# A hybrid attention and HGRN2 layer: weight differences, q and k evictions and output weights put at other places in the engines' order

## The chip, the cores and the metric

The kernel runs on one core of one Trainium2 chip. The time is the device time of one launch in microseconds (us); three runs of the kernel before gave 1321.59, 1317.43 and 1322.69, median 1321.59. The engines are called PE (TensorE, matmuls), PEld (its weight loads), DVE (VectorE), ACT (ScalarE), POOL (GpSimd) and SP (SyncE, which here issues the DMAs).

## The reference

One decoder layer over 1040 tokens (16 meta tokens ahead of 1024), model width 1024, float32:

```python
a = rmsnorm(h, ln_mix_pre[l])
proj = a @ w_in[l]
dq, dk, dv, hq, hf, hi, hg = jnp.split(proj, SPLITS, axis=-1)
y_diff = diff_attention(dq, dk, dv, ...)      # 4 heads: softmax(q0 k0) - lam * softmax(q1 k1), times v, rmsnorm
y_hgrn = hgrn2(hq, hf, hi, hg, ...)           # 4 heads of gated linear recurrence
mix = jnp.concatenate([y_diff, y_hgrn], axis=-1) @ w_out[l]
h = h + rmsnorm(mix, ln_mix_post[l])
a = rmsnorm(h, ln_ffn_pre[l])
y = conv_ffn(a, w_ffn_up[l], ffn_conv_w[l], ffn_conv_b[l], w_ffn_down[l])   # width 2816, causal conv of 3
h = h + rmsnorm(y, ln_ffn_post[l])
```

The output is h without the meta tokens.

## The kernel before

Every float32 operand of a large product is split into a high and a low part in a faster format, and a product is three matmuls (high·high, high·low, low·high). The feed-forward part uses a Strassen-like scheme with fewer products of 512-wide halves; for that it needs differences of pieces of `w_down`, which are made early, beside the projections, and kept in DRAM (`tsc`).

The tokens are nine blocks: one of 16 and eight of 128, in three groups (`GROUPS`, 272, 384 and 384 tokens). The input projection is 28 tiles of 128 columns, each a set of three groups. Tiles named `dq`, `dk`, `dv` feed an attention head, `hq`, `hf`, `hi`, `hg` an HGRN2 head. While the projection of the next head runs, the current head is computed: `interleave` takes steps of the head (a generator that yields a cost) and fills PE between them with projection matmuls. Attention heads 0 to 3 and HGRN2 heads 0 to 3 alternate. After HGRN2 head 3 comes the output projection with `w_out`, in two column halves, the first of them beside HGRN2 head 3 (`out_first`); then the feed-forward part, to the end.

PE executes in the order in which the program is written. The other engines are put in order by a scheduler, which goes by the order of writing as a priority and by when it thinks operands are ready. Two means restrict it: `tc.keep_in_program_order`, which the class `Ordered` applies to DVE's and ACT's instructions while `state["ordered"]` is set, and `with tc.issue_after(ins)`, which puts what stands in the block behind `ins` on its engine. All DVE and ACT instructions go through `Ordered`, so that the profile gives them one line, L54; they are told apart by tile names.

The names that matter here:

- `down_sums` (L195 on) is a generator advanced once for each projection group. For each of 11 rounds it loads four 128x512 pieces of `w_down` (`wd11`, `wd12`, `wd22`, `wd21`, in a pool of five buffers), makes four differences on DVE (`wd3` = 22 − 12, then 12, 22 and 21 in place), and stores each to `tsc` by SP.
- `ev_q` and `ev_k` evict a PSUM bank of the q or k projection (`pi_dq`, `pi_dk`, two banks in turn): ACT writes the scaled or rounded copy, DVE the remainder. For k the remainder goes to a tile `kl`, and ACT writes a second copy into the other half of the partitions.
- `attn` runs, for each block i, the scores (`scores`), the transposes of its softmax weights `pb` into `at` (`values`, matmuls on L693) and their product with v (`apply`, L717).
- In an HGRN2 head, level 1 to 7 of a tree each need `mix` and `kr` scaled by DVE (`mix<-mix,tt`, `kr<-kr,tt`) before their matmuls `pl<-mix,kr` on L459; `a` and `am` receive the masked result.
- `load_wo` loads a 128x512 piece of `w_out` into a buffer `wor` (three in turn) and splits it: a cast on ACT (`wh` or `woh`), the remainder on DVE (`wl` or `wol`). `mm` are the split activations of the output projection, `py` its sums.

Of the kernel before, what the change touches and what calls it, by code (L numbers as in the profile page):

```python
# [13 lines left out]
ALU = mybir.AluOpType  # L14
# [8 lines left out]
KD = D // P  # L23
# [3 lines left out]
NBLK = 9  # L27
# [18 lines left out]
class Ordered:  # L46
# [3 lines left out]
    def __getattr__(self, name):  # L50
        call = getattr(self.engine, name)

        def issue(*args, **kw):
            ins = call(*args, **kw)  # L54
            return self.tc.keep_in_program_order(ins) if self.state["ordered"] else ins

        return issue
# [29 lines left out]
def layer_kernel(ctx: ExitStack, tc: tile.TileContext, x, meta, table, lbl, gpre, gpost, win,  # L87
# [3 lines left out]
    V, A = Ordered(tc, nc.vector, state), Ordered(tc, nc.scalar, state)  # L91
# [56 lines left out]
    def ps_m(name):  # L148
        return pp.tile([P, 512], F32, tag="m", name=name)
# [4 lines left out]
    def split(hi, lo, raw, eng=None):  # L154
        A.copy(hi, raw)
        (eng or G).tensor_tensor(lo, raw, hi.bitcast(F32), op=ALU.subtract)
# [38 lines left out]
    def down_sums():  # L195
        def load(k):
            with tc.issue_after(last_load[-1].ins):
                for nm, kk, half in (("11", k, 0), ("12", k, 1), ("22", k + NF // 2, 1), ("21", k + NF // 2, 0)):
                    b[nm] = wsp.tile([P, 512], F32, tag="wd", name=f"wd{nm}_{k}")
                    SY.dma_start(b[nm], wdown[P * kk: P * (kk + 1), 512 * half: 512 * (half + 1)])  # L200
            b["t3"] = wsp.tile([P, 512], F32, tag="wd", name=f"wd3_{k}")

        b = {}
        load(0)
        yield
        yield
        for k in range(NF // 2):
            for j, d, p_, q_ in ((2, "t3", "22", "12"), (0, "12", "12", "11"), (1, "22", "22", "12"), (3, "21", "21", "22")):
                V.tensor_tensor(b[d], b[p_], b[q_], op=ALU.subtract)
                with tc.issue_after(last_load[-1].ins):  # L210
                    SY.dma_start(tsc[j][P * k: P * (k + 1)], b[d])
                yield
            if k + 1 < NF // 2:
                load(k + 1)
                yield

    def up_raw(ft, nm):
# [374 lines left out]
    def attn_in(h):  # L592
        qs = [ap_.tile([P, L], F32R, tag=f"q{m}", name=f"q{m}_{h}") for m in range(2)]
        ks = [ap_.tile([P, L], F32R, tag=f"k{m}", name=f"k{m}_{h}") for m in range(2)]
        vn = ap_.tile([P, NBLK, P], F32, tag="avn", name=f"avn{h}")
        G.memset(vn[:, 0], 0.0)
        rr = ap_.tile([P, 256], F32, tag="rr", name=f"rr{h}")
        own = [slice(0, 64), slice(64, 128)]
        oth = [slice(64, 128), slice(0, 64)]

        def ev_q(g, b0, b1, t0, t1, pt):
            for m in range(2):
                A.mul(qs[m][own[m], t0:t1], pt[own[m]], 0.125)
                V.scalar_tensor_tensor(qs[m][oth[m], t0:t1], pt[own[m]], 0.125, qs[m][own[m], t0:t1].bitcast(F32), ALU.mult, ALU.subtract)

        def ev_k(g, b0, b1, t0, t1, pt):
            for m in range(2):
                A.copy(ks[m][own[m], t0:t1], pt[own[m]])
                V.tensor_tensor(kl[m][own[m], t0:t1], pt[own[m]], ks[m][own[m], t0:t1].bitcast(F32), op=ALU.subtract)
                A.copy(ks[m][oth[m], t0:t1], pt[own[m]])  # L610

        def ev_v(g, b0, b1, t0, t1, pt):
            vt = ap_.tile([P, 384], F32, tag="vt", name=f"vt{h}_{g}", bufs=1)
            A.copy(vt[:, : t1 - t0], pt)
            late.append((vn, vt, b0, b1, f"va{h}_{g}"))

        return (qs, ks, vn, rr), [(h, f"dq{h}", ev_q), (4 + h, f"dk{h}", ev_k), (8 + h, f"dv{h}", ev_v)]

    def attn(h, tens):
        qs, ks, vn, rr = tens  # L620
# [115 lines left out]
        for i in range(NBLK):  # L736
            if i + 2 < NBLK:
                ahead = scores(i + 2)
                yield next(ahead)
            yield from apply(i)  # L740
            if i + 2 < NBLK:
                yield from ahead
            if i + 2 == NBLK:
                yield 2
            if i + 1 < NBLK:
                yield from values(i + 1)
        carry.append(pend.pop("tail"))
# [42 lines left out]
    pt = ps_m("pg")  # L790
# [80 lines left out]
    for c in range(2):  # L871
        raw = wp.tile([P, 512], F32, tag="wr", name=f"wr3_{c}", bufs=3)
# [61 lines left out]
    FIRST = (2, 3, 4, 5, 6, 7, 8, 1)  # L934
    kept = kpp.tile([P, 2, KD, P], F32R, tag="kept", name="kept")

    def load_wo(n, k):
        raw = wp.tile([P, 512], F32, tag="wr", name=f"wor{n}_{k}", bufs=3)
        last_load.append(SY.dma_start(raw, wout[P * k: P * (k + 1), 512 * n: 512 * (n + 1)]))
        if k < 2:  # L940
            where, tag, bufs = wp, ("wh", "wl"), 4
        elif n == 0 and k < KD - 1:
            where, tag, bufs = w0p, ("woh", "wol"), KD - 3
        else:
            where, tag, bufs = w1p, ("woh", "wol"), KD - 1
        hi, lo = (where.tile([P, 512], F32R, tag=t, name=f"{t}{n}_{k}", bufs=bufs) for t in tag)
        split(hi, lo, raw, V if n or k else G)
        return hi, lo
# [41 lines left out]

    sps = [mix_split(i, 0, 4) for i in FIRST[:2]]
    mix_split(0, 0, 7)
    wo0 = [load_wo(0, k) for k in range(KD)]
    wo = []

    pre_last = {}
# [27 lines left out]
    def out_first():  # L1024
        pys = [ps_s(f"py0_{i}")[:, 0] for i in FIRST[:2]]
        for ks in ((0, 1), (2, 3)):
            for j in range(2):
                yield from out_part(sps[j], pys[j], wo0, ks[0] == 0, False, ks)
        sqs = [mix_split(i, 4, 7) for i in FIRST[:2]]
        for j in range(2):  # L1030
            yield from out_part(sqs[j], pys[j], wo0, False, True)
            if j == 0:
                sp_ = mix_split(FIRST[2], 0, 4)
            A.copy(y0[:, FIRST[j]], pys[j])
        for n, i in enumerate(FIRST[2:]):
            for k in ((0, 1), (2, 3), (4,), (5,), (6,), (7,))[n]:
                wo.append(load_wo(1, k))
            if n == 3:
                ahead.extend(mix_load(2, c) for c in range(4))
            py = ps_in(f"py0_{i}")  # L1040
            sq_ = mix_split(i, 4, 7)
            yield from out_part(sp_, py, wo0, True, False)
            if i != FIRST[-1]:
                sp_ = mix_split(FIRST[n + 3], 0, 4)
            yield from out_part(sq_, py, wo0, False, True)
            A.copy(y0[:, i], py)
        py = ps_in("py0_0")
        yield from out_meta(py, wo0, 0, 7, 6)
        A.copy(y0[:2, 0], py[32:34])
        V.tensor_tensor(y0[:2, 0], y0[:2, 0], py[:2], op=ALU.add)  # L1050
        while 0 not in finished:
            yield None
        for p in range(3):
            pre_last[p] = mix_split(p, 7, 8)
        for p in range(3):
            yield from out_last(p)
# [171 lines left out]
    for n, i in enumerate(order):  # L1228
# [9 lines left out]
        nxt = []  # L1238
# [521 lines left out]
```

## Time and profile before

| | before |
|---|---|
| median of three runs | 1321.59 us |
| the profiled execution: its own time | 1323.17 us |
| its span | 1321.4 us |
| PE busy | 1273.0 us, 96% |
| DVE busy | 920.0 us, 70% |
| ACT busy | 689.2 us, 52% |
| POOL busy | 419.0 us, 32% |

A row of the timeline gives the start in us from the span's start, the length, engine, source line, operation, output tile <- input tiles, shapes, and how many were grouped; in brackets how long the engine stood idle before it and whose result ended that. A row of the waits gives an engine's instruction, what it waited for, the sum in us, how often, and the longest. A row by windows gives the stretch and its length, then for each engine its busy time with the number of instructions.

The projection with heads beside it takes the first 500 us or so; the output projection lies up to about 560 us; the feed-forward part, which the change does not touch, follows.

### The profile page before, as it was taken

How to read it: one execution, taken by the hardware profiler on the slowest of the kernel's cores; microseconds unless marked ns; L12 is line 12 of the kernel's file. 1: busy time of each engine (PE TensorE's matmuls, PEld its weight loads, DVE VectorE, ACT ScalarE, POOL GpSimd, SP SyncE). 2: the span in 40 equal slices, each digit the busy share in tenths (PEclk: the TensorE clock that was granted, in tenths of full speed). 3: DMA queues.
4: the chain of work that ended last, by engine and by line, in shares of the span. 5: the costliest groups of instructions: out<-in, count | busy, mean ns of one | idle time of the engine just before them, and what ended most of it. 6: DMA issues, size and time to landing. Idle time of an engine off the chain costs nothing.

```text
span 1321.4 us, 26287 instructions
## 1 busy us (share of the span) xinstructions
PE 1273.0 (96%) x10212; PEld 1180.3 (89%) x10212; DVE 920.0 (70%) x1591; ACT 689.2 (52%) x1671; POOL 419.0 (32%) x325
## 2 busy tenths in 40 slices
PE   6999999999999999999999989999999999999997
PEld 5898899989999999777899989999999998888886
DVE  7566556564756465746889877877787875697587
ACT  7365346535654565456655444455454453554454
POOL 3211211121202120113156757667666641010021
PEclk9999999999999999999999989999999999999999
DMA  6331323142311111836613222222222325964363
GB/s 218 106 130 61 100 93 129 61 129 80 122 44 35 33 33 49 255 112 206 226 41 113 89 80 88 80 83 79 81 89 80 105 81 163 355 216 155 109 207 120
DMA packets 84371, 153.07 MB, mean 116 GB/s; under 512 B 9571, under 2 KB 19843, under 8 KB 84246
## 3 DMA queue, kind: packets, MB, share of 16 engines
q1 hardware_dynamic: 84246, 151.39, 34.6%
q8 instruction: 80, 1.31, 0.4%
q14 instruction: 45, 0.37, 0.1%
HBM read 112.69 MB, written 38.67 MB: 115 GB/s over the span
## 4 chain that ended last, share of the span: by engine, by line
PE 64%; DVE 7%; issue 2%; ACT 2%; DMA 2%; SPq 0%; POOL 0%; DVEq 0%; ACTq 0%; POOLq 0%
PE pd L1571 5%; PE pd L1572 5%; PE pd L1570 5%; PE pb L1360 4%; PE pb L1361 4%; PE pb L1362 4%; PE pa L1361 2%; PE pa L1360 2%; PE pa L1362 2%; PE pc L1362 2%; PE pc L1360 2%; PE pc L1361 2%; DVE c L54 2%; PE py L978 2%; PE pa L717 2%
## 5 line engine op out<-in xcount | busy, mean ns | idle before, releaser
L1360 PE MATMUL pb<-t,uh 128*128 128x258 f32 (+1 forms) x480 | 135.7, 283 | 10.3 <-DVE u L54 10.3
L1361 PE MATMUL pb<-t,uh 128*128 128x258 f32 (+1 forms) x480 | 135.2, 282 | 0.0
L1362 PE MATMUL pb<-t,ul 128*128 128x258 f32 (+1 forms) x480 | 135.1, 281 | 0.0
L1572 PE MATMUL pd<-wh,gl 128*128 128x512 f32 (+1 forms) x314 | 121.0, 385 | 0.0
L1571 PE MATMUL pd<-wl,gh 128*128 128x512 f32 (+1 forms) x314 | 120.5, 384 | 0.4 <-DVE wl L54 0.3
L1570 PE MATMUL pd<-wh,gh 128*128 128x512 f32 (+1 forms) x314 | 120.8, 385 | 0.0
L54 DVE SCALAR_TENSOR_TENSOR c<-uu,cwt,c 128x512 f32<-128x512 f32 x88 | 96.5, 1097 | 19.8 <-ACT c L54 19.2
L1306 POOL TENSOR_TENSOR c<-c,c 128x512 f32<-128x512 f32 x44 | 67.6, 1536 | 118.4 <-ACT c L54 112.3
L1360 PEld LDWEIGHTS pb<-t,uh 128*128 128x128 f32 x480 | 91.5, 191 | 11.1 <-DVE u L54 11.1
L54 DVE SCALAR_TENSOR_TENSOR c<-ug,cwt,c 128x512 f32<-128x512 f32 x88 | 89.8, 1020 | 2.9 <-ACT c L54 2.3
L1361 PEld LDWEIGHTS pb<-t,uh 128*128 128x128 f32 x480 | 91.6, 191 | 0.0
L1362 PEld LDWEIGHTS pb<-t,ul 128*128 128x128 f32 x480 | 91.5, 191 | 0.0
L1361 PE MATMUL pa<-t,uh 128*128 128x258 f32 (+1 forms) x320 | 89.9, 281 | 0.0
L1360 PE MATMUL pa<-t,uh 128*128 128x258 f32 (+1 forms) x320 | 89.8, 281 | 0.0
L1362 PE MATMUL pa<-t,ul 128*128 128x258 f32 (+1 forms) x320 | 89.8, 280 | 0.0
L1362 PE MATMUL pc<-t,ul 128*128 128x256 f32 x320 | 88.3, 276 | 0.0
L1360 PE MATMUL pc<-t,uh 128*128 128x256 f32 x320 | 88.3, 276 | 0.0
L1361 PE MATMUL pc<-t,uh 128*128 128x256 f32 x320 | 88.3, 276 | 0.0
L1571 PEld LDWEIGHTS pd<-wl,gh 128*128 128x128 f32 x314 | 58.9, 188 | 14.1 <-DVE wl L54 1.6
L1572 PEld LDWEIGHTS pd<-wh,gl 128*128 128x128 f32 x314 | 59.0, 188 | 12.1
L1570 PEld LDWEIGHTS pd<-wh,gh 128*128 128x128 f32 x314 | 59.0, 188 | 11.5
L54 ACT ACTIVATE pb<-S,ast 128x528 f32<-128x528 f32 (+7 forms) x72 | 46.6, 648 | 39.2 <-DVE ast L54 39.1
(411 smaller groups left out, 4210.8 us busy)
## 6 DMA issues: line engine op xcount, KB each, us to landing
ra<-in_wup_dram SPq DMA_DIRECT2D x80, 256.0 KB, 2.7
wd<-in_wdown_dram SPq DMA_DIRECT2D x44, 256.0 KB, 4.6
tsc<-wd SPq DMA_DIRECT2D x44, 256.0 KB, 2.9
gsc<-c SPq DMA_DIRECT2D x44, 256.0 KB, 2.0
wi<-tsc SPq DMA_DIRECT2D x44, 256.0 KB, 3.0
gi<-gsc SPq DMA_DIRECT2D x33, 256.0 KB, 4.2
wi<-in_wdown_dram SPq DMA_DIRECT2D x33, 256.0 KB, 3.3
msc<-mm SPq DMA_DIRECT2D x21, 256.0 KB, 3.7
```

Of the source, the lines that this page charges most:

```text
L54: ins = call(*args, **kw)
L717: T.matmul(po[:, :P], w_, vn[:, j], start=(j == 0), stop=(j == i))
L978: T.matmul(py[:r], mh[:, j, :r], hi, start=(first and j == 0), stop=False)
L1306: G.tensor_tensor(cg, cg, cu, op=ALU.mult)
L1360: T.matmul(pt, hi[:, s], th[:, k], start=(first and k == 0), stop=False, skip_group_check=True)
L1361: T.matmul(pt, hi[:, s], tl[:, k], start=False, stop=False, skip_group_check=True)
L1362: T.matmul(pt, lo[:, s], th[:, k], start=False, stop=(k == 3), skip_group_check=True)
L1570: T.matmul(py, gh[:, s], wh, start=(k == 0 and pr not in (3, 7)), stop=False, skip_group_check=True)
L1571: T.matmul(py, gh[:, s], wl, start=False, stop=False, skip_group_check=True)
L1572: T.matmul(py, gl[:, s], wh, start=False, stop=(k == NH - 1), skip_group_check=True)
```

## The change

Four places are edited. (1) Each difference of `down_sums` is written inside `issue_after(V.last.ins)`, that is behind the DVE instruction written last before it, and a round has one yield more, so a round takes six projection groups instead of five. (2) `ev_q` writes both ACT copies before both DVE remainders; `ev_k` writes all four ACT copies before both DVE remainders. (3) In `attn`, a yield of 1 is added ahead of the last block's `apply`, and one of 2 becomes 3 ahead of its `values`. (4) `load_wo` is parted into the load (`load_wr`) and the split; for the second column half the load is written one block earlier than the split, and the split is written behind the DVE instruction before it.

```diff
         def issue(*args, **kw):
             ins = call(*args, **kw)
+            self.last = ins
             return self.tc.keep_in_program_order(ins) if self.state["ordered"] else ins
...
         for k in range(NF // 2):
             for j, d, p_, q_ in ((2, "t3", "22", "12"), (0, "12", "12", "11"), (1, "22", "22", "12"), (3, "21", "21", "22")):
-                V.tensor_tensor(b[d], b[p_], b[q_], op=ALU.subtract)
+                with tc.issue_after(V.last.ins):
+                    V.tensor_tensor(b[d], b[p_], b[q_], op=ALU.subtract)
                 with tc.issue_after(last_load[-1].ins):
                     SY.dma_start(tsc[j][P * k: P * (k + 1)], b[d])
                 yield
             if k + 1 < NF // 2:
                 load(k + 1)
+                yield
                 yield
...
             for m in range(2):
                 A.mul(qs[m][own[m], t0:t1], pt[own[m]], 0.125)
+            for m in range(2):
                 V.scalar_tensor_tensor(qs[m][oth[m], t0:t1], pt[own[m]], 0.125, qs[m][own[m], t0:t1].bitcast(F32), ALU.mult, ALU.subtract)
...
             for m in range(2):
                 A.copy(ks[m][own[m], t0:t1], pt[own[m]])
+                A.copy(ks[m][oth[m], t0:t1], pt[own[m]])
+            for m in range(2):
                 V.tensor_tensor(kl[m][own[m], t0:t1], pt[own[m]], ks[m][own[m], t0:t1].bitcast(F32), op=ALU.subtract)
-                A.copy(ks[m][oth[m], t0:t1], pt[own[m]])
...
+            if i + 1 == NBLK:
+                yield 1
             yield from apply(i)
             if i + 2 < NBLK:
                 yield from ahead
             if i + 2 == NBLK:
-                yield 2
+                yield 3
...
-    def load_wo(n, k):
+    def load_wr(n, k):
         raw = wp.tile([P, 512], F32, tag="wr", name=f"wor{n}_{k}", bufs=3)
         last_load.append(SY.dma_start(raw, wout[P * k: P * (k + 1), 512 * n: 512 * (n + 1)]))
+        return n, k, raw
+
+    def load_wo(n, k, raw):
...
-    wo0 = [load_wo(0, k) for k in range(KD)]
+    wo0 = [load_wo(*load_wr(0, k)) for k in range(KD)]
...
+        nxt = [load_wr(1, k) for k in (0, 1)]
         for n, i in enumerate(FIRST[2:]):
-            for k in ((0, 1), (2, 3), (4,), (5,), (6,), (7,))[n]:
-                wo.append(load_wo(1, k))
+            for w in nxt:
+                with tc.issue_after(V.last.ins):
+                    wo.append(load_wo(*w))
+            nxt = [load_wr(1, k) for k in ((2, 3), (4,), (5,), (6,), (7,), ())[n]]
```

How this moves instructions, at three places. First DVE in HGRN2 head 0, beside the dq projection of attention head 1 (`wd..._3` are pieces of the fourth round, `wd3_2` one of the third, `q0`/`q1` the q remainders, `f0`, `tt0` the factors of levels 1 and 2). Before:

```order
L54 TENSOR_TENSOR wd12_3_1976<-wd12_3_1976,wd11_3_1974 128x512
L54 TENSOR_TENSOR wd22_3_1978<-wd22_3_1978,wd12_3_1976 128x512
L54 TENSOR_TENSOR mix1_100<-mix1_100,f0_738 128x192
L54 TENSOR_TENSOR kr0_739<-kr0_739,f0_738 128x520
L54 TENSOR_TENSOR mix0_99<-mix0_99,f0_738 128x136
L54 TENSOR_TENSOR mix2_101<-mix2_101,f0_738 128x192
L54 COPY_PREDICATED a320_1641<-mask_732,pl0_1_1718 128x128
L54 COPY_PREDICATED am_736<-mask_732,pl0_1_1718 16x8
L54 TENSOR_TENSOR wd21_3_1980<-wd21_3_1980,wd22_3_1978 128x512
L54 SCALAR_TENSOR_TENSOR q0_1_1591<-pi_dq1_1_1699,q0_1_1591 64x384
L54 TENSOR_TENSOR mix1_100<-mix1_100,tt0_1639 128x96x2
```

and after:

```order
L54 TENSOR_TENSOR mix1_100<-mix1_100,f0_738 128x192
L54 TENSOR_TENSOR mix2_101<-mix2_101,f0_738 128x192
L54 TENSOR_TENSOR kr0_739<-kr0_739,f0_738 128x520
L54 TENSOR_TENSOR mix0_99<-mix0_99,f0_738 128x136
L54 COPY_PREDICATED a320_1639<-mask_732,pl0_1_1714 128x128
L54 COPY_PREDICATED am_736<-mask_732,pl0_1_1714 16x8
L54 SCALAR_TENSOR_TENSOR q0_1_1582<-pi_dq1_1_1695,q0_1_1582 64x384
L54 SCALAR_TENSOR_TENSOR q1_1_1583<-pi_dq1_1_1695,q1_1_1583 64x384
L54 TENSOR_TENSOR wd3_2_1621<-wd22_2_1617,wd12_2_1615 128x512
L54 TENSOR_TENSOR kr0_739<-kr0_739,tt0_1637 128x260x2
L54 TENSOR_TENSOR mix0_99<-mix0_99,tt0_1637 128x68x2
```

The pair ahead of level 1 and the single piece behind it are gone from there; one piece of the round before stands between the two q remainders and the `kr` of level 2.

Second, ACT at the k evictions of the same head (`k0`, `k1` the two copies, `wh_hf` weight casts, `kn` a copy of transposed k). Before:

```order
L54 CAST k0_1_1593<-pi_dk1_1_1983 64x384
L54 CAST wh_hf1_0_2327<-wr_hf1_0_2326 128x512
L54 CAST k0_1_1593<-pi_dk1_1_1983 64x384
L54 CAST k1_1_1594<-pi_dk1_1_1983 64x384 x2
L54 CAST wh_hf1_1_2333<-wr_hf1_1_2332 128x512
L54 CAST k0_1_1593<-pi_dk1_2_2081 64x384
L54 COPY kn0_0_2136<-pk0_0_2137 128x384
L54 CAST k0_1_1593<-pi_dk1_2_2081 64x384
L54 CAST k1_1_1594<-pi_dk1_2_2081 64x384 x2
```

and after:

```order
L54 CAST k0_1_1584<-pi_dk1_1_1972 64x384 x2
L54 CAST k1_1_1585<-pi_dk1_1_1972 64x384 x2
L54 CAST wh_hf1_0_2321<-wr_hf1_0_2320 128x512
L54 CAST wh_hf1_1_2327<-wr_hf1_1_2326 128x512
L54 CAST k0_1_1584<-pi_dk1_2_2070 64x384 x2
L54 CAST k1_1_1585<-pi_dk1_2_2070 64x384 x2
L54 COPY kn0_0_2132<-pk0_0_2133 128x384
```

The four casts of a bank now stand together, the weight casts and `kn` behind them.

Third, DVE in the output projection, HGRN2 head 3, levels 1 and 2. Before:

```order
L54 COPY_PREDICATED am_736<-mask_732,pl3_1_6494 16x8
L54 TENSOR_TENSOR wl1_1_6550<-wor1_1_6547,wh1_1_6549 128x512
L54 TENSOR_TENSOR wol1_2_6674<-wor1_2_6671,woh1_2_6673 128x512
L54 TENSOR_TENSOR mm5_4_6684<-mix1_100,mm5_4_6684 128x384
L54 TENSOR_TENSOR kr3_5484<-kr3_5484,tt3_6413 128x260x2
L54 TENSOR_TENSOR mix0_99<-mix0_99,tt3_6413 128x68x2
```

and after:

```order
L54 COPY_PREDICATED am_736<-mask_732,pl3_1_6494 16x8
L54 TENSOR_TENSOR wl1_0_6546<-wor1_0_6541,wh1_0_6545 128x512
L54 TENSOR_TENSOR wl1_1_6550<-wor1_1_6543,wh1_1_6549 128x512
L54 TENSOR_TENSOR mm5_4_6686<-mix1_100,mm5_4_6686 128x384
L54 TENSOR_TENSOR kr3_5478<-kr3_5478,tt3_6413 128x260x2
L54 TENSOR_TENSOR mix0_99<-mix0_99,tt3_6413 128x68x2
```

`wol1_2` no longer stands ahead of level 2; it comes behind level 3. `wl1_0`, which stood ahead of level 1, takes a place behind it.

## The prediction

> **What bounds the kernel now.** I read the page's first rows, then the waits of TensorE (PE) in the part of the span that the change touches, then stage lengths, and only then single instructions. The page:
>
> ```profile
> span 1321.4 us, 26287 instructions
> PE 1273.0 (96%) x10212; PEld 1180.3 (89%) x10212; DVE 920.0 (70%) x1591; ACT 689.2 (52%) x1671; POOL 419.0 (32%) x325
> tsc<-wd SPq DMA_DIRECT2D x44, 256.0 KB, 2.9
> ```
>
> PE is busy in 1273.0 of 1321.4 us, and the change takes no matmul away. So only PE's idle time can be won, 48.4 us in the whole span. The last row is the 44 stores of the w_down differences: 44 subtractions on VectorE (DVE) stand behind it. The edits lie ahead of 560 us; there PE waits as follows (waited for, sum in us, times, longest):
>
> ```profile
> PE pl L459 <- DVE mix L54: 5.7, 6, 2.0
> PE px L279 <- DVE xs L54: 3.9, 5, 1.8
> PE pt L693 <- DVE at L54: 2.3, 4, 1.0
> PE pa L717 <- ACT pb L54: 1.9, 3, 0.8
> PE pi_dv L240 <- DVE q L54: 1.7, 1, 1.7
> PE pi_dv L240 <- ACT k L54: 1.5, 3, 0.5
> PE pi_hf L240 <- ACT k L54: 1.1, 1, 1.1
> PE pl L459 <- DVE am L54: 0.7, 1, 0.7
> ```
>
> The first row is the largest: a level of the HGRN2 tree waits until DVE has scaled `mix`. The two `k` rows and the `q` row are evictions that hold up the next projection. The `xs` row belongs to the opening, which the change leaves alone.
>
> How much of this belongs to the subtractions is seen by comparing equal stages. Three heads run the same program beside the dq and dk projections of the next attention head, and the last of them has no `wd` work. The first three rows are dq beside HGRN2 heads 0, 1, 2 (each from the first matmul of that projection to the first of the next), the next three dk, the last four hq beside attention heads 0 to 3. Columns: window, length, then busy time of PE, weight loads, DVE, ACT, POOL, and clock, DMA share, GB/s.
>
> ```profile
> 142.98:160.83 17.85, 15.61 (x341) 14.16 (x341) 12.84 (x28) 5.11 (x10) 2.95 (x5) 1.00 0.51 164
> 273.17:289.88 16.71, 15.56 (x340) 14.19 (x340) 12.51 (x28) 5.11 (x10) 2.92 (x5) 1.00 0.69 222
> 402.57:418.06 15.49, 15.45 (x341) 14.16 (x340) 10.29 (x26) 5.12 (x10) 3.39 (x6) 1.00 0.12 36
> 160.83:176.30 15.47, 15.38 (x251) 14.00 (x250) 12.47 (x32) 7.29 (x17) 3.88 (x6) 1.00 0.14 40
> 289.88:306.69 16.81, 15.81 (x251) 14.19 (x250) 15.09 (x36) 7.30 (x17) 4.90 (x7) 1.00 0.15 39
> 418.06:433.54 15.48, 15.39 (x252) 14.00 (x251) 11.96 (x31) 7.30 (x17) 3.45 (x5) 1.00 0.15 46
> 81.51:102.19 20.68, 19.36 (x132) 18.57 (x132) 15.59 (x35) 12.39 (x38) 4.48 (x4) 1.00 0.56 192
> 211.69:230.54 18.85, 18.03 (x122) 17.05 (x122) 14.52 (x35) 13.07 (x46) 4.84 (x4) 1.00 0.47 154
> 341.72:359.96 18.24, 18.01 (x122) 17.06 (x122) 14.87 (x35) 13.12 (x44) 4.83 (x4) 1.00 0.47 161
> 468.54:485.98 17.44, 17.44 (x122) 17.11 (x122) 12.02 (x26) 12.40 (x39) 4.81 (x4) 1.00 0.10 33
> ```
>
> In the first dq window the `wd` subtractions alone (length, DVE busy; the control has none):
>
> ```profile
> 142.98:160.83 17.85, 2.82 (x4) 1.00 0.51 164
> ```
>
> The clock is 1.00 in all of them. Four subtractions, 2.82 us of DVE, go with 2.36 us more length: a burst ahead of a chain that PE waits for costs nearly its own duration. Alone, the subtractions would be 0.7 us each.
>
> **The subtractions, one in a group.** Before, DVE took several in a row wherever the loads let it (here in head 0 at level 1, between the q eviction and the `mix` that level 1 needs):
>
> ```profile
> 152.42 1.42 DVE L54 TENSOR_TENSOR wd<-wd,wd 128x512 f32<-128x512 f32 x2
> 155.07 0.69 PE L459 MATMUL pl<-mix,kr 128*32 128x16 f32 x62 [1.61 <-DVE mix L54]
> ```
>
> The burst of two is 1.42 us, PE's wait is 1.61. After, each subtraction is pinned behind the DVE instruction last written, which puts at most one in a projection group, and the additional yield makes a round of weights six groups, not five. The bursts go. If the three disturbed stages come to the control's length, that is (17.85 − 15.49) + (16.71 − 15.49) + (16.81 − 15.48) = 4.9 us. The work itself does not go: it now also lands in HGRN2 head 2 and in attention head 3, which had none. Whether one subtraction fits is decided by the control's own slack at its tightest level:
>
> ```profile
> 412.36 0.48 ACT L54 ACTIVATE q<-pi_dq 64x384 fp32r<-64x384 f32 x1 [2.53 <-PE pi_dq L244]
> 412.88 0.55 DVE L54 SCALAR_TENSOR_TENSOR q<-pi_dq,q 64x384 fp32r<-64x384 f32 x1 [0.87 <-ACT q L54]
> 414.84 0.70 DVE L54 TENSOR_TENSOR kr<-kr,tt 128x520 f32<-128x520 f32 x1
> 415.46 0.30 DVE L54 TENSOR_TENSOR mix<-mix,tt 128x136 f32<-128x136 f32 x1
> 416.41 0.70 PE L459 MATMUL pl<-mix,kr 128*32 128x16 f32 x62
> ```
>
> DVE ends the chain at 415.76 and PE starts level 2 at 416.41: 0.65 us of slack. The changed order there is q0, q1, `wd`, `kr`, three `mix`. With both ACT casts first (412.36 + 2 × 0.48 = 413.3), q0 and q1 at 0.55 each and a pass between engines, `wd` at 0.61 (rows of two next to each other, 1.42 for 0.71 + 0.71, overlap by about 0.1 with what follows), `kr` 0.61 and three `mix` at some 0.3, the chain ends near 416.6. So a wait of about 0.2 us appears at level 2 of each of three heads: −0.6 us. Bounds: 0 (the slack holds) and a whole piece of 0.71 for each, 2.1 us. I take 0.2, since the control's rows give it. Net of this part in the dq and dk stages: +4.3.
>
> [...] The single rows here show 0.69, but neighbours in this trace start 0.61 apart. [...]
>
> The hq stages show the same burden as PE idle time inside the window: (20.68 − 19.36) + (18.85 − 18.03) + (18.24 − 18.01) = 2.4, against 0.0 in the last head. That goes too. Attention head 3 now gets some eight subtractions over its stages and its neighbours a steady one per group; for what they delay in the attention chains I take 0.5 (bounds 0 and eight times 0.15, 1.2: DVE there is busy 12.02 of 17.44, so most of them find a hole). Net +1.9.
>
> **The k and q evictions.** Head 0, the last dk group, in the order of time on three engines (two rows of it left out):
>
> ```profile
> 176.79 0.47 ACT L54 CAST k<-pi_dk 64x384 fp32r<-64x384 f32 x1
> 179.30 0.56 DVE L54 TENSOR_TENSOR kl<-pi_dk,k 64x384 fp32r<-64x384 f32 x1 [1.41 <-ACT k L54]
> 179.90 0.48 ACT L54 CAST k<-pi_dk 64x384 fp32r<-64x384 f32 x1 [0.63 <-DVE kl L54]
> 180.42 0.44 PE L240 MATMUL pi_dv<-ahi,wh_dv 128*128 128x384 f32 x1 [0.50 <-ACT k L54]
> ```
>
> The bank passes between the engines: cast, subtract, two casts, subtract, cast, from 176.79 to 180.38. With four casts first and both subtractions after: 176.77 + 4 × 0.48 = 178.7, + 2 × 0.55 = 179.8, before PE's next need at 179.92 (180.42 less the wait of 0.50). The three waits on `k` (1.5 us) go. So does the single wait of 1.1 in front of `pi_hf`, which came from three subtractions in a row ahead of a `kl`. Sum +2.6; bounds 0 (another engine's hand-over takes the place) and 2.6. Moved behind the casts are the `kn` copy (about 178.8 to 179.2, used by PE past 180.5) and two weight casts that are needed a stage later: nothing. On DVE the second `kl` now ends no later than before.
>
> The q edit shows in one place, the first projection:
>
> ```profile
> 24.29 0.43 DVE L54 SCALAR_TENSOR_TENSOR q<-pi_dq,q 64x272 fp32r<-64x272 f32 x1
> 24.75 1.42 DVE L54 SCALAR_TENSOR_TENSOR xs<-xt,ss,gb 128x512 f32<-128x512 f32 x2
> 26.20 0.44 DVE L54 SCALAR_TENSOR_TENSOR q<-pi_dq,q 64x272 fp32r<-64x272 f32 x1
> 26.79 0.37 PE L240 MATMUL pi_dv<-ahi,w 128*128 128x272 f32 x1 [1.70 <-DVE q L54]
> ```
>
> The second q no longer stands behind 1.42 us of `xs`; PE's wait of 1.70 falls to about 0.3. But `xs` moves back by 0.44, DVE has no pause there, and PE waits for `xs` a moment later. I take +0.7, the middle of 0 and 1.4 to 1.7, because the opening is bound by DVE.
>
> **Output weights one block ahead.** Two waits stand there:
>
> ```profile
> 545.02 0.62 ACT L54 CAST woh<-wor 128x512 fp32r<-128x512 f32 x1 [3.56 <-DMA wor<-in_wout_dram]
> 545.67 0.69 DVE L54 TENSOR_TENSOR wol<-wor,woh 128x512 fp32r<-128x512 f32 x1 [3.31 <-ACT woh L54]
> 547.80 0.91 PE L459 MATMUL pl<-mix,kr 128*32 128x16 f32 x62 [2.01 <-DVE mix L54]
> ```
>
> DVE stands 3.31 us behind a cast that waits for its load, with `kr` and `mix` of level 2 behind it, and PE pays 2.01. With the raw load issued a block earlier and the split pinned after level 3, that goes, and so does the 0.7 on `am`: 2.7. Against it, the loads of first-half pieces 5 to 7 are pushed behind two stores on SP's queue and I expect a new wait of 0.5 to 1.4 at piece 6. Net +1.3 (bounds 0.5 and 2.7).
>
> **The attention yields** shift the projection work by one step about the last two blocks. PE's order ahead of the waits on `at` and `pb` (2.3 + 1.9) does not change in it: 0.
>
> **SP's queue.** The stores and loads of the later `wd` rounds now stand ahead of some weight loads. The smallest slack I find is a hf weight issued near 292 in the dk stage that ends at 306.69, 14 us. Nothing.
>
> **The sum.** 4.3 + 1.9 + 2.6 + 0.7 + 1.3 = 10.8. A wait costs PE a little beyond its idle time: in the three dq and dk stages the lengths shrink by 4.9 us where idle time shrinks by 4.2 (length less PE's busy time, 2.24 + 1.15 + 1.00 against 0.04, 0.04 and 0.09), 0.7 over some five waits, 0.15 each. For eight more waits that no stage length holds that is 1.2. Together −12.0 us. The profiled execution took 1323.17 us against a median of 1321.59, so its own time would become 1311.2 and the median 1309.6. About 0.5% (6.6 us) is what a measurement of this kernel can tell from no change.
>
> **The rivals.**
>
> - *The waits only move.* The subtractions remain 44 × 0.7 = 31 us of DVE work, and head 2 and attention head 3, idle-free so far, take their share. If each new place gives back 0.2 to 0.7 us and the evictions find another hand-over, 0 to 6.6 us remain, in the middle 3.3: 1318. For it: slack of 0.65 against a piece of 0.61 to 0.71. Against it: bursts of two to five cost much more than single pieces in the rows above.
> - *Slower: every pinned piece heads a chain.* Each subtraction now stands at a fixed place on DVE, ready or not, and all behind it waits. If the places have less slack than a piece is long, 44 × 0.61 = 26.8 us come on, less the 12 gained: 1336. It decides once the slack at a place falls below 0.61; 0.65 is the tightest I saw.
> - *A late weight.* A store stands on SP until its subtraction is done, with a weight load behind it. Beyond 14 us of slack each further us costs PE one; at some 20 us 1329. The DMA's 2.9 us for a store speaks against it.
> - *The yields help too.* If the additional filler lies ahead of the waits on `at` and `pb`, 4.2 us go as well: 1305.4.
>
> **How the numbers follow.** The forecast, 0.70; yields too, 0.06; waits only move, 0.18; slower by chains 0.03, by a late weight 0.03. The prediction is the first, 1309.6. The range reaches down to 1304.5, which takes in the yields' case and the sum of the upper bounds (4.9 + 2.4 + 2.6 + 1.7 + 2.7 + 1.2 = 15.5, 1306.1), and up to 1317.0, where little more than the first term, 4.3, is left. Faster by over 0.5% are the first two cases, 0.76; the third counts as the same, 0.18; slower 0.06.
>
> **What would show it.** Right: PE's row on `mix` falls from 5.7 to under 2; the two rows on `k` vanish; the dq windows of all three heads lie between 15.5 and 15.9; DVE's busy sum stays near 920. Wrong on the first step: level 2 waits over 0.5 in all heads, or new rows of PE on `at` in attention head 3. Wrong on the output weights: a new wait on `wol` of over 1.4. Wrong altogether: PE waiting for a DMA of a projection weight.

## The result and the profile after

The changed kernel took 1311.42 us (median of six, 1310.32 to 1313.40), the kernel before 1320.99 in the six runs beside it: ratio 0.9926, 95% interval 0.9911 to 0.9941, or 9.6 us less. The forecast was 12.0 less, 1309.6, range 1304.5 to 1317.0.

The first rows of the page after:

```profile
span 1311.6 us, 26288 instructions
PE 1270.9 (97%) x10212; PEld 1180.8 (90%) x10212; DVE 923.1 (70%) x1591; ACT 691.1 (53%) x1671; POOL 416.9 (32%) x325
```

DVE's work is the same, 923.1 us against 920.0. PE's idle time fell from 48.4 to 40.7 us. Where PE still waits in the first 560 us, the rows that bear on the change (waited for, sum, times, longest):

```profile
PE pt L698 <- DVE at L54: 2.3, 4, 1.0
PE pl L462 <- DVE mix L54: 2.1, 3, 0.7
PE pa L722 <- ACT pb L54: 1.9, 3, 0.8
PE pi_dv L243 <- DVE kl L54: 1.9, 3, 0.7
PE py L988 <- ACT woh L54: 1.4, 1, 1.4
PE pk L518 <- DVE kr L54: 1.4, 1, 1.4
PE pi_dv L243 <- DVE q L54: 0.2, 1, 0.2
PE py L990 <- DVE wol L54: 0.2, 1, 0.2
```

The `mix` row shrank from 5.7 to 2.1, but all three of its waits are new ones at a fixed place. The two rows on `k` (1.5 and 1.1) are gone, and a row on `kl` (1.9) stands in their place; the `q` row fell from 1.7 to 0.2. Two rows of 1.4 in the output projection are new. The rows on `at` (2.3) and `pb` (1.9) are what they were. Three rows of the attention heads in the kernel before, 2.4 us together, have gone:

```profile
PE pa L717 <- DVE at L54: 1.2, 3, 0.8
PE pa L717 <- ACT ona L54: 0.6, 1, 0.6
PE ssa L577 <- DVE ona L54: 0.6, 1, 0.6
```

The stages by windows (length, then busy time of PE, PEld, DVE, ACT, POOL, then clock, DMA share, GB/s): the three dq stages, then hq beside attention heads 0 to 3.

```profile
137.78:154.43 16.65, 15.80 (x341) 14.32 (x341) 11.96 (x27) 5.11 (x10) 4.58 (x8) 1.00 0.30 98
264.80:281.46 16.66, 15.81 (x340) 14.34 (x340) 13.16 (x29) 5.11 (x10) 4.04 (x7) 1.00 0.50 157
391.57:408.25 16.68, 15.83 (x341) 14.35 (x340) 11.97 (x27) 5.12 (x10) 4.04 (x7) 1.00 0.22 68
78.58:97.79 19.21, 19.14 (x133) 18.63 (x133) 14.64 (x31) 12.66 (x39) 4.06 (x4) 1.00 0.44 138
204.73:222.17 17.44, 17.44 (x122) 17.11 (x122) 12.92 (x29) 12.33 (x38) 4.87 (x4) 1.00 0.15 47
331.51:348.94 17.43, 17.43 (x122) 17.11 (x122) 13.93 (x30) 12.39 (x38) 5.16 (x4) 1.00 0.43 139
458.56:476.00 17.44, 17.44 (x123) 17.11 (x122) 12.04 (x27) 12.33 (x38) 4.88 (x4) 1.00 0.13 33
```

The hq stages now have no idle time to speak of (17.44 busy of 17.44, where before 18.03 of 18.85). The dq stages are all alike at 16.66: the first gained 1.2 us, the second nothing, and the third, the control, lost 1.2.

The rest of the text needs one table of all kernels. It is worked out from PE's timeline: each stage reaches from the first matmul of a projection to that of the next; the last two columns are the output projection (from the last matmul of the input projection to the first of the feed-forward's up products) and those up products. Times in us, one profiled execution each.

| kernel | first dq+dk | first dv | dq, 3 heads | dk, 3 | dv, 3 | hq+hi, 4 | output | up |
|---|---|---|---|---|---|---|---|---|
| before | 15.2 | 39.6 | 50.1 | 47.8 | 60.0 | 170.7 | 123.3 | 450.4 |
| after | 13.7 | 38.3 | 50.0 | 45.6 | 60.0 | 166.0 | 124.5 | 449.5 |
| part 1 alone | 15.2 | 39.1 | 49.9 | 46.4 | 67.1 | 166.0 | 124.1 | 448.1 |
| part 2 alone | 13.9 | 39.0 | 48.9 | 49.0 | 59.4 | 172.1 | 123.9 | 449.5 |
| part 3 alone | 15.3 | 39.5 | 48.4 | 49.9 | 60.0 | 173.0 | 123.2 | 449.9 |
| part 4 alone | 15.3 | 39.0 | 48.8 | 48.9 | 60.0 | 171.9 | 121.3 | 447.3 |
| parts 1 and 2 | 13.8 | 38.6 | 50.0 | 45.6 | 60.0 | 166.0 | 124.7 | 448.4 |
| parts 1, 2 and 4 | 13.9 | 38.3 | 50.0 | 45.6 | 60.0 | 166.0 | 121.1 | 447.8 |
| the same, dv split later | 13.8 | 38.4 | 46.8 | 45.9 | 60.0 | 166.0 | 121.4 | 447.4 |
| and hf cast later | 14.0 | 38.4 | 46.8 | 46.0 | 57.9 | 166.0 | 120.5 | 447.6 |

The gain of the changed kernel lies ahead of the output projection: 1.5 + 1.3 + 0.1 + 2.2 + 0.0 + 4.7, and 0.3 in stages that are not listed; from PE's timeline 10.0 in all. The output projection lost 1.2, the up products came out 0.9 shorter. This last number is no effect of the change that could be traced: the column moves between 447.3 and 450.4 over kernels that are alike there.

One caution on this table. The kernel with part 4 alone has the same order of instructions as the kernel before on every engine up to 538 us, and yet its dq, dk and hq+hi stages differ by 1.3, 1.1 and 1.2 us. So among the rows without part 1 such differences are no effect of a part, and the 4.7 gained in hq+hi is the low end of 4.7 to 7.0 over these rows; dq and dk together keep within 97.7 and 98.3. The rows with part 1 repeat: hq+hi is 166.0 in every one.

### The profile page after: what moved, and what is told of

It reads as the page before. It is cut to its first block, busy times and chain, and to the rows that moved or that the text cites. A ratio compares the mean times of both kernels' runs of the same rounds, so it can differ in the third digit from the quotient of the medians.

```text
span 1311.6 us, 26288 instructions
## 1 busy us (share of the span) xinstructions
PE 1270.9 (97%) x10212; PEld 1180.8 (90%) x10212; DVE 923.1 (70%) x1591; ACT 691.1 (53%) x1671; POOL 416.9 (32%) x325
## 4 chain that ended last, share of the span: by engine, by line
PE 83%; DVE 9%; DMA 2%; issue 2%; ACT 2%; POOL 0%; SPq 0%; DVEq 0%; ACTq 0%; POOLq 0%
PE pd L1585 5%; PE pd L1584 5%; PE pd L1583 5%; PE pb L1373 4%; PE pb L1374 4%; PE pb L1375 4%; PE pa L722 3%; PE pa L1374 2%; PE pa L1373 2%; PE pa L1375 2%; DVE c L54 2%; PE pc L1375 2%; PE pc L1374 2%; PE pc L1373 2%; PE py L988 2%
## 5 line engine op out<-in xcount | busy, mean ns | idle before, releaser
L1585 PE MATMUL pd<-wh,gl 128*128 128x512 f32 (+1 forms) x314 | 121.1, 386 | 0.0
L1583 PE MATMUL pd<-wh,gh 128*128 128x512 f32 (+1 forms) x314 | 120.9, 385 | 0.0
L1584 PE MATMUL pd<-wl,gh 128*128 128x512 f32 (+1 forms) x314 | 120.5, 384 | 0.4 <-DVE wl L54 0.3
L1584 PEld LDWEIGHTS pd<-wl,gh 128*128 128x128 f32 x314 | 59.0, 188 | 13.9 <-DVE wl L54 1.5
L157 POOL TENSOR_TENSOR ul<-ws,uh 128x512 fp32r<-128x512 f32 x40 | 56.4, 1410 | 26.0 <-ACT uh L54 26.0
```

What stands on the lines that cost most here:

```text
L1583: T.matmul(py, gh[:, s], wh, start=(k == 0 and pr not in (3, 7)), stop=False, skip_group_check=True)
L1584: T.matmul(py, gh[:, s], wl, start=False, stop=False, skip_group_check=True)
L1585: T.matmul(py, gl[:, s], wh, start=False, stop=(k == NH - 1), skip_group_check=True)
```

## Experiments: each part alone

Four kernels, each the kernel before with one part of the change, told apart how the gain is made up.

**Part 1 alone.**

```diff
+                with tc.issue_after(V.last.ins):
+                    V.tensor_tensor(b[d], b[p_], b[q_], op=ALU.subtract)
...
                 load(k + 1)
                 yield
+                yield
```

> The kernel before with part 1 alone (each w_down difference behind the DVE instruction written last, a round of six groups). Theory, read from the trace after: this part carries most of the gain, about -7 us (hq stages of heads 0 to 2 at 17.4, 17.4 and 19.2 us, no wait of 1.1 ahead of pi_hf), but the dq stages of all three HGRN2 heads end at 16.6 us, because the piece moves three mix operations under a POOL weight split of 1.29 us and they take 2.1 us instead of 0.83. Rival, the prediction's sizing: VectorE pieces alone set the level 2 wait, 0.2 us each, dq stages 15.5 to 15.9 us, total -7.5 us with 4.3 from dq and dk.

Measured: 1321.68 us beside 1323.87 for the kernel before, ratio 0.9986 (0.9973 to 1.0000), 2.2 us less by the medians, with an interval that just reaches no change. Both sizes were far off. The hq stages came out as expected, 4.7 us shorter with hi. But the dv stages became 7.1 us longer. PE's waits in that kernel between 35 and 520 us, its first two rows:

```profile
PE pi_dv L243 <- ACT k L54: 5.4, 3, 1.8
PE pl L462 <- DVE mix L54: 3.3, 3, 1.1
```

The waits on `k` rose from 3 times 0.5 to 3 times 1.8. The chain in head 0 on DVE, POOL and ACT shows why:

```profile
171.56 0.69 DVE L54 TENSOR_TENSOR wd<-wd,wd 128x512 f32<-128x512 f32 x1
172.77 1.44 DVE L54 TENSOR_TENSOR mix<-mix,tt 128x192 f32<-128x192 f32 x1
172.64 1.36 POOL L157 TENSOR_TENSOR wl_hf<-wr_hf,wh_hf 128x512 fp32r<-128x512 f32 x1 [2.12 <-ACT wh_hf L54]
174.84 0.54 DVE L54 TENSOR_TENSOR kl<-pi_dk,k 64x384 fp32r<-64x384 f32 x1
175.41 0.96 ACT L54 CAST k<-pi_dk 64x384 fp32r<-64x384 f32 x2 [1.33 <-DVE kl L54]
176.40 0.56 DVE L54 TENSOR_TENSOR kl<-pi_dk,k 64x384 fp32r<-64x384 f32 x1 [1.02 <-ACT k L54]
```

A piece of `wd` at 171.56 stands ahead of the first `kl`, ACT cannot go on with its casts until that `kl` is made, and so the hand-overs of the old eviction order pass the delay on. The piece is the smaller part of the delay: it takes 0.61 until the next operation starts, and it moves `mix` beside a POOL weight split, where `mix` takes 1.44 us; in the kernel before the same `mix` ended ahead of that split and took 0.35 (at 176.38). From one `kl` to the next DVE now needs 3.31 us (171.53 to 174.84) where it needed 1.61 (175.74 to 177.35), and 0.61 and 1.09 make up the 1.70. The section on the level 2 wait tests this collision. After the wait there is a second loss: PE's clock. By windows of the same execution (columns as above, the clock third from the end):

```profile
179.00:182.00 3.00, 3.00 (x13) 2.90 (x12) 0.69 (x2) 0.48 (x1) 0.00 (x0) 0.51 0.00 0
183.00:186.00 3.00, 3.00 (x25) 3.00 (x24) 0.79 (x3) 1.54 (x9) 0.00 (x0) 1.00 0.00 0
```

From 179 to 182 the granted clock is 0.51, and PE does 13 matmuls in 3 us where it does 25 a little later. The dv stage of that head is 22.9 us for 20.0. The third head gives the parting: there PE stops for the same 1.82 us ahead of 437.94, the clock stays at 1.00, and the stage is 21.3. So 1.3 are the longer wait and 1.6 the clock.

**Part 2 alone.** The new `ev_q` and `ev_k` as in the diff of the change.

> The kernel before with part 2 alone (all ACT copies of a q or k bank first, then the DVE remainders). Theory: the first projection gains 1.4 us, the k banks gain nothing (the waits of 0.5 on k come back as waits on kl of 0.4 to 0.7, because the two DVE remainders now come last and stand behind mix operations that a POOL split holds up): about -1.5 us. Rival, the prediction's sizing: the k waits go too, -3.3 us.

Measured: 1322.39 beside 1323.87, ratio 0.9989 (0.9979 to 1.0000). The interval takes in the theory's 1.5 us, and its places hold: the first dq and dk stages are 1.3 us shorter, and the dv stages 0.6, with waits of 0.43, 0.42 and 0.43 us on `kl` in place of 0.5 on `k`. The forecast of −3.3 lies outside the interval.

**Part 4 alone.** `load_wr` and `load_wo` as in the diff of the change.

> The kernel before with part 4 alone (raw loads of the second column half one block earlier, split behind the DVE instruction before it). Theory: level 2 of HGRN2 head 3 no longer waits 2.0 us, but the last piece's cast on ACT waits for its load, an mm remainder waits for that on DVE, and PE waits about 1.4 us at pk for kr; no wait on woh near 527: about -1.0 us. Rival, the prediction's sizing: pushed first-half pieces give a wait of 0.5 to 1.4 at woh or wol, and no wait at pk: -1.3 us with the wait there.

Measured: 1321.65 beside 1323.87, ratio 0.9986 (0.9974 to 0.9998). The output projection is 2.0 us shorter, 121.3. Both were wrong on what comes instead: there is no wait at `pk`, none at `woh` and none on `mix`; PE waits 0.7 on `am` there, and 0.5 ahead of a level for nothing that the profile shows.

**Part 3 alone.** The two yields of `attn`.

> The kernel before with part 3 alone (the two attention yields). Theory: the yields, not the output weights' part, put two msc stores and the gpo load ahead of first-half weight pieces 5 to 7 on SP's queue; a wait of about 1.4 us on woh at the output projection's piece 5 or 6 appears and the time rises by 1 to 1.5 us. Rival, the prediction's: nothing, 0 us, waits on at and pb unchanged and none on woh.

Measured: 1322.83 beside 1323.87, ratio 0.9995 (0.9982 to 1.0007): no difference, as the rival said. But the places are the theory's. PE's waits in the output projection of that kernel:

```profile
PE pk L515 <- DVE kr L54: 1.4, 1, 1.4
PE py L980 <- ACT woh L54: 0.3, 1, 0.3
PE py L982 <- DVE wol L54: 0.2, 1, 0.2
```

The yields alone move the weights: the 2.0 at `mix` is gone there too, and 1.4 at `pk` and 0.5 at `woh` and `wol` have come. It is about even when part 4 is absent. With part 4, which removes the 2.0 by itself, only the cost is left. In the longer dk stages of this kernel in the table the granted clock fell to 0.52 behind a stop of 2.07 us ahead of 293.88.

## Experiments: what the parts do together

**Without the yields** (parts 1, 2 and 4; the forecasts call this kernel k1).

```diff
-            if i + 1 == NBLK:
-                yield 1
...
-                yield 3
+                yield 2
```

> The changed kernel without part 3 (the two attention yields). Theory, from the run of the yields alone: in the changed kernel they do nothing but put the first-half weight pieces 5 to 7 later on SP's queue and the last level's kr behind a late weight; without them the waits of 1.41 and 0.23 us at woh and wol and of 1.36 us at pk go, and the time is 2.5 to 3 us below the changed kernel's (ratio to before about 0.9905). Rival, the prediction's: the yields are worth 0, ratio 0.9926 as for the changed kernel, and the waits stay because part 4 makes them.

Measured: 1308.95 beside 1323.38, ratio 0.9887 (0.9872 to 0.9902), an interval that lies clear of the changed kernel's 0.9911 to 0.9941. By the ratios that is some 5 us; the traces place 3.4 of it: the output projection takes 121.1 where it takes 124.5 with the yields. Its only wait there that the trace shows:

```profile
PE py L986 <- ACT mm L54: 0.9, 1, 0.9
```

So the yields make the waits at `woh`, `wol` and `pk`, and part 4 does not. SP's queue in the changed kernel shows the way: a store of `mm` and the load `gpo` are issued ahead of the weight pieces that PE wants next, and ACT then stands for a load with an `mm` cast behind it. The first three rows and the last are the changed kernel's, the one in between is SP's without the yields; the last projection matmul starts at 517.92 in the one and at 518.50 in the other.

```profile
518.45 0.63 SPq L931 DMA_DIRECT2D gpo<-in_gpost_dram  x1
519.12 0.51 SPq L979 DMA_DIRECT2D msc<-mm  x1
519.73 1.53 SPq L946 DMA_DIRECT2D wor<-in_wout_dram  x3
...
517.86 0.56 SPq L944 DMA_DIRECT2D wor<-in_wout_dram  x1
...
526.15 1.93 ACT L54 CAST woh<-wor 128x512 fp32r<-128x512 f32 x3 [3.06 <-DMA wor<-in_wout_dram]
```

**Parts 1 and 2 together.** The two diffs above in one kernel.

> The kernel before with parts 1 and 2 together. Theory, the two parts need each other: part 1 alone lengthens the k bank's hand-overs (waits of 1.8 us at pi_dv in three heads), which part 2 shortens to 0.4 to 0.7, and part 2 puts both q remainders ahead of the piece; together about -7.5 us (ratio 0.994). Rival, the parts add up: -2.2 and -1.5 make -3.7 us (ratio 0.9975).

Measured: 1313.19 beside 1323.38, ratio 0.9923 (0.9911 to 0.9936). The theory is right on the direction and still too small: alone the parts gain 0.14% and 0.11%, together 0.77%. Part 1 moves the waits from the attention stages to the k banks; part 2 takes the hand-overs away through which they would grow there: dv stages 60.0 in place of 67.1. These two parts alone gain as much as the whole change (0.9926).

**The pin without the yield of `down_sums`, and the yield without the pin**, both on the kernel without the attention yields. The first:

```diff
                 load(k + 1)
                 yield
-                yield
```

> As k1_no_yields, with the pin but without the additional yield of a round (a round of five groups again). Theory: the pin alone spreads the subtractions, so the hq stages stay at 17.4 to 19.2 us and the time within 2 us of k1's (ratio 0.9875 to 0.990); it differs only by which levels a piece now meets. Rival: without the sixth group the next round's loads are late, pieces wait for their DMA on DVE with chains behind them, and half of part 1's gain goes (ratio 0.992 or more).

Measured: 1309.26 beside 1324.83, ratio 0.9884 (0.9862 to 0.9906): the same as with the yield. The second:

```diff
-                with tc.issue_after(V.last.ins):
-                    V.tensor_tensor(b[d], b[p_], b[q_], op=ALU.subtract)
+                V.tensor_tensor(b[d], b[p_], b[q_], op=ALU.subtract)
```

> As k1_no_yields, with the additional yield but without the pin. Theory: the subtractions go back into bursts of three and four, hq stages rise above 18 us for heads 1 and 2 and PE's waits on mix, ona and at come back: 4 to 6 us above k1 (ratio 0.992 to 0.9935). Rival: the longer round, not the pin, made the gain; ratio as k1's, 0.989.

Measured: 1312.45 beside 1324.83, ratio 0.9906 (0.9887 to 0.9925). The interval overlaps that of the kernel with pin and yield (0.9872 to 0.9902). Beside the pin alone, on the same chip, the medians differ by 3.2 us and no run of the one reaches a run of the other (1311.58 to 1313.97, 1307.86 to 1310.55); that is less than expected. Of this some 2 us are the output projection (122.9 for 120.9), where no subtraction stands any more, so the trace does not give them to the pin. Ahead of it the hq stages of heads 0 and 1 are 19.6 and 17.9 us for 19.2 and 17.4, and a wait of 0.6 on `ona` is back: only a part of the burden returned. The pin suffices without the yield. That the yield without the pin does part of it is argued from this run; parts 2 and 4 with neither were not run.

## Experiments: the level 2 wait and the kl wait

In the changed kernel, head 0, level 2 on DVE and PE, and the weight split on POOL:

```profile
149.73 0.69 DVE L54 TENSOR_TENSOR wd<-wd,wd 128x512 f32<-128x512 f32 x1
150.34 0.69 DVE L54 TENSOR_TENSOR kr<-kr,tt 128x520 f32<-128x520 f32 x1
150.95 2.12 DVE L54 TENSOR_TENSOR mix<-mix,tt 128x136 f32<-128x136 f32 x3
...
152.65 0.86 PE L462 MATMUL pl<-mix,kr 128*32 128x16 f32 x48 [0.71 <-DVE mix L54]
...
151.08 1.29 POOL L157 TENSOR_TENSOR wl_dv<-wr_dv,wh_dv 128x512 fp32r<-128x512 f32 x1 [11.26 <-ACT wh_dv L54]
```

Three `mix` operations take 2.12 us; in the experiment below the same three take 1.05. The difference is 1.07, and POOL's split of 1.29 ran from 151.08 to 152.37. Without it the last `mix` would have ended about 152.0, as PE came to need it: the wait of 0.71 ends at 152.65, so PE stood from 151.94. Not every DVE operation is longer beside a split: in the kernel before, the `kl<-pi_dk,k` at 177.35 took 0.54 us inside a POOL split that ran from 176.85 to 178.13, and the one at 179.30, with no split beside it, 0.56. What sets `mix` and `kl` apart in this, no run shows.

**POOL's dv split behind the tree's halvings.**

```diff
-        (eng or G).tensor_tensor(lo, raw, hi.bitcast(F32), op=ALU.subtract)
+        with tc.issue_after(halves[-1].ins) if behind else nullcontext():
+            (eng or G).tensor_tensor(lo, raw, hi.bitcast(F32), op=ALU.subtract)
```

(`behind` is set for the dv weights; `halves` holds the halvings on POOL. The next forecast calls this kernel k2.)

> As k1, and POOL's remainder of the first dv weight of each tile put behind the tree's last halving on POOL. Theory, the two engines block each other: the three mix operations of level 2 fall from 2.1 us to 0.8, PE's waits of 0.71 us in the middle of level 2 go in all three heads, dq stages 15.5 to 15.8 us in place of 16.65, about -3 us against k1. Rival, the w_down piece alone fills the slack: dq stages stay above 16.3, at most -0.5 us against k1.

Measured: 1306.12 beside 1323.38, ratio 0.9874 (0.9860 to 0.9887). Against k1, on the same chip, the median is 2.8 us less, but the intervals overlap; the timeline and the dq stages by windows are clear:

```profile
151.04 1.05 DVE L54 TENSOR_TENSOR mix<-mix,tt 128x136 f32<-128x136 f32 x3
```

```profile
137.87:153.46 15.59, 15.55 (x341) 14.26 (x341) 10.90 (x27) 5.11 (x10) 3.43 (x8) 1.00 0.27 87
264.10:279.70 15.60, 15.56 (x340) 14.27 (x340) 12.10 (x29) 5.11 (x10) 3.44 (x8) 1.00 0.50 171
390.29:405.90 15.61, 15.57 (x340) 14.28 (x340) 10.91 (x27) 5.11 (x10) 3.43 (x8) 1.00 0.26 86
```

The `wd` piece is still at level 2 in all three heads; the orders of PE, DVE, ACT and SP are the same in both kernels, only POOL's differs, and 1.06 us of each stage went. That shows the cause. The piece seems to be needed for the collision too: in the kernel with the pin alone, where no piece falls on level 2 of head 2, that stage is 15.5 us. But there POOL also does three halvings ahead of its split, so the piece's share is argued, not shown: 0.61 us later, the last two `mix` lie under the split.

**ACT's hf casts behind the k casts**, in addition.

```diff
-        A.copy(hi, raw)
+        with tc.issue_after(kcast[-1].ins) if late else nullcontext():
+            A.copy(hi, raw)
...
-                A.copy(ks[m][oth[m], t0:t1], pt[own[m]])
+                kcast.append(A.copy(ks[m][oth[m], t0:t1], pt[own[m]]))
```

(`late` is set for the hf weights.)

> As k2, and ACT's casts of the hf weights put behind the k casts that are written ahead of them, which moves POOL's remainders of them too. Theory: the two kl remainders no longer stand behind a mix and a wd piece that a POOL split holds up, and PE's waits on kl at pi_dv (0.72, 0.42, 0.73 us) go: about -2 us against k2, ratio to before about 0.987. Rival: the waits come from the order of four casts and two remainders itself (3.0 us of work behind 3.1 us of cover) and stay within 0.2 us of what they were.

Measured: 1304.31 beside 1323.38, ratio 0.9858 (0.9845 to 0.9872), the fastest version of this study. Against the kernel with the dv split moved, on the same chip, the median is 1.8 us less and no run of the one reaches a run of the other. The dv stages fell by 2.1 us, and the row on `kl` is gone from PE's waits. In the changed kernel first, then in this one, the two `kl` and what stands ahead:

```profile
168.19 1.36 DVE L54 TENSOR_TENSOR wd<-wd,wd 128x512 f32<-128x512 f32 x1
170.28 1.71 DVE L54 TENSOR_TENSOR mix<-mix,tt 128x192 f32<-128x192 f32 x2
172.61 1.11 DVE L54 TENSOR_TENSOR kl<-pi_dk,k 64x384 fp32r<-64x384 f32 x2
173.87 0.41 PE L243 MATMUL pi_dv<-ahi,wh_dv 128*128 128x384 f32 x1 [0.72 <-DVE kl L54]
```

```profile
168.12 0.69 DVE L54 TENSOR_TENSOR wd<-wd,wd 128x512 f32<-128x512 f32 x1
169.53 0.62 DVE L54 TENSOR_TENSOR mix<-mix,tt 128x192 f32<-128x192 f32 x2
171.70 1.13 DVE L54 TENSOR_TENSOR kl<-pi_dk,k 64x384 fp32r<-64x384 f32 x2 [0.86 <-ACT k L54]
```

and ACT's casts in the changed kernel:

```profile
169.69 0.62 ACT L54 CAST wh_hf<-wr_hf 128x512 fp32r<-128x512 f32 x1 [2.04 <-POOL wl_hf L157]
170.34 1.93 ACT L54 CAST k<-pi_dk 64x384 fp32r<-64x384 f32 x4
```

A `wd` of 1.36 became 0.69, and two `mix` of 1.71 became 0.62. The `kl` now wait for ACT's casts and end at 172.83, before PE needs the bank. So the order of four casts and two remainders does fit its cover, as the forecast reckoned. What did not fit was the hf work beside it, in two ways: POOL's split of 1.38 us at 170.39, beside which the two `mix` took 1.71, so that DVE came to the `kl` only at 172.61, and ACT's hf cast of 0.62, which stood ahead of the four `k` casts, so that they ended at 172.27. With DVE free at that moment the two `kl` would still have ended near 173.4, where PE stood from 173.15: by this estimate about 0.3 of the 0.72 would have stayed for the cast alone. The edit moves casts and splits together, and no run parts the two.

## Why the prediction was right, and where not

- **The total** was 12.0 us of gain, measured 9.6. Ahead of the output projection the steps sum to 4.3 + 1.9 + 2.6 + 0.7 + 1.2 = 10.7, measured 10.0. The sum is nearly right, its terms are not: dq and dk fell 2.0 short, hq and hi came out 2.8 above, and that the two cancel is luck.
- **dq and dk stages**: +4.3 forecast, 2.3 measured (0.1 + 2.2 in the table). The step that failed is the level 2 wait, taken as 0.2 in each head: it was 0.71 and, in a second stop, 0.09. This is the sign that the prediction had named for its first step being wrong (level 2 waits over 0.5 in all heads, dq windows outside 15.5 to 15.9). The chain on DVE was costed with durations from the control, where POOL's split came after it, and without POOL. Without that collision the dq stages are 15.6, inside the 15.5 to 15.9 forecast. Rows of the kernel before already showed what a split does to two `mix`, 1.57 us where two others took 0.63 (at 156.87):

```profile
159.54 1.29 POOL L156 TENSOR_TENSOR wl_dv<-wr_dv,wh_dv 128x512 fp32r<-128x512 f32 x1
159.84 1.57 DVE L54 TENSOR_TENSOR mix<-mix,t 128x192 f32<-128x192 f32 x2 [0.32 <-POOL tt L423]
```

- **hq stages**: +1.9 forecast, 4.7 with hi. The term left out the hi stage (1.0), allowed 0.5 for new waits that did not come, and counted only idle time inside the hq windows, 2.4, where the whole shortening is 3.7. The rest is busy time that went too (19.36 to 19.14, 18.03 to 17.44, 18.01 to 17.43), which the prediction had in its separate 1.2 for what a wait costs beyond idle time, against its first paragraph, by which only idle time could be won.
- **k evictions**: +2.6 forecast. The wait of 1.1 ahead of `pi_hf` went (first dv stage 1.3 shorter); the three on `k` came back as 1.9 on `kl`, dv stages 60.0 as before. The calculation (casts to 178.7, remainders to 179.8) took DVE to be free at 178.7 and ACT to start on the bank at once; DVE stood behind two `mix` that took 1.71 us beside a POOL split (0.62 where the hf casts and splits were moved), and ACT behind an hf cast of 0.62, which the prediction had put at nothing. What the part is really worth was not among the steps: it is the condition for part 1, since alone part 1 gains 2 us and costs 7.1 in the dv stages.
- **First q eviction**: +0.7 forecast as the middle of 0 and 1.7; measured 1.5 on the first dq and dk stages (1.3 with part 2 alone), near the upper bound. The `xs` that move back cost less than assumed.
- **Output weights**: +1.3 forecast, and the output projection became 1.2 longer. The term itself had the right sign and was too small: part 4 alone shortens that stage by 2.0 (123.3 to 121.3), and on top of parts 1 and 2 by 3.6 (124.7 to 121.1). The late pieces 5 to 7 and a wait of 0.5 to 1.4 were forecast and came (1.41 and 0.23). But they were put down to part 4, and they belong to the yields; the second new wait, 1.36 at `pk`, was missed.
- **Attention yields**: 0 forecast. The step failed: the order of PE ahead of the waits on `at` and `pb` was looked at, and those waits did stay (2.3 and 1.9), but not what the shift does to SP's queue behind them. It costs 3.4 us in the output projection, the largest single error; without the yields the gain was 14.4 us (1308.95 beside 1323.38).
- **The rivals**: "the waits only move" was right for the k banks and for level 2, wrong for the attention stages. "The yields help too" had the wrong sign. Nothing of the slower cases came.

## What to carry to other kernels

Pinning background work one piece at a time paid here, where a burst used to stand ahead of a chain that PE waits for (hq and hi stages 166.0 us in place of 170.7). But look for the next hand-over that has no slack: here part 1 alone gained almost nothing (2.2 us) until the evictions stopped passing a bank back and forth (dv stages 60.0 in place of 67.1). Cost each chain with what the neighbouring engine does at that moment, POOL beside DVE here (three `mix` in 2.12 us in place of 1.05), and follow a small shift in the order of writing through every queue, DMA issue among them (3.4 us in the output projection here).

## What the runs showed of the hardware

In the kernel before, one float32 matmul of 384 columns (`pb<-oh,tbb` at 48.19) held PE for 0.83 us, to the start of the next matmul; three matmuls of the split form with 384 columns each (`pi_dq`, from 49.31) took 0.52.

Three `mix` on DVE took 2.12 us beside a POOL split of 1.29, and 1.05 with the split moved; a `wd` took 1.36 beside a split of 1.28 (at 167.73 in the changed kernel), and 0.69 where the hf casts and splits were moved. The `kl` inside a split took 0.54, the one without 0.56.

And a stop of PE cost more than itself here. In the kernel with part 1 alone, the stop of 1.82 us ahead of 177.52 was followed by a granted clock of 0.51 from 179 to 182, which cost 1.6 us on top. Not each stop of this length does it. In the same kernel, the window from 2 to 5 us behind the stop of 1.82 us ahead of 437.94:

```profile
440.00:443.00 3.00, 3.00 (x24) 2.96 (x23) 0.22 (x1) 0.52 (x2) 0.00 (x0) 1.00 0.00 0
```

The clock is 1.00 there, as it is behind the stop of 2.01 us in the kernel before (ahead of 547.80). What decides was not found here.
